# Seven products for eight: Strassen's scheme over pairs of weight blocks in a four-mixer decoder layer

## The chip, the cores and the metric

The kernel runs on one core of one Trainium2 chip. The metric is the device time of one execution in microseconds (us), and lower is better. The work of a core is spread over TensorE (PE: matmuls; PEld is its loading of the stationary operand), VectorE (DVE), ScalarE (ACT) and GpSimd (POOL), with DMA queues that SyncE (SP) and GpSimd fill. Each engine takes its instructions in program order and waits on semaphores for the others.

## The reference

One pre-norm residual layer over 256 tokens of width 2048, in float32. What matters here is the shape of the products: `h @ w_in` is 256 x 2048 by 2048 x 17,492, four branch products are 256 x 512 by 512 x 2048, and the output projection is 256 x 2048 by 2048 x 2048.

```python
h = rms_norm(x, norm_w)
p = h @ w_in
z, gate, dsa_qkv, idx_q, idx_k, idx_w, fox_qkv, fox_f, diff_qkv, dil_qkv = split(p)
branches = (dsa_attention(...), forgetting_attention(...),          # 4 heads of 128
            differential_attention(...), dilated_attention(...))
for b in range(4):
    y = branches[b] * silu(z_parts[b])                              # 256 x 512
    term = sigmoid(g_parts[b]) * (y @ w_branch[b])                  # 256 x 2048
    merged = term if merged is None else merged + term
x = x + merged @ w_out
return rms_norm(x, final_norm_w)
```

The first mixer scores all keys with a 16-head indexer and keeps the best 64. The second adds cumulative log forget gates. The third is the difference of two softmaxes a head. The fourth is a dilated window. Three of them add a position bias.

## The kernel before

Every product has float32 precision made of two parts: an operand is split in a high part (rounded to the format that TensorE multiplies at full rate) and a low part (the rest), and high x high, low x high and high x low are summed in PSUM. The activations are split once (`hT`, 16 chunks of 128 input columns by 256 tokens). The weights pass by in units: a `Unit` is a block of 4 chunks of 128 rows by 512 columns, 1 MB. `load` issues its DMA on the SP queue into one of four buffers `raw`; `split` lets ScalarE copy the high part `whi` (L134) and VectorE subtract it to get the low part `wlo` (L135). High and low parts have three buffers each (`SPLIT + 1`).

There are two forms of products. In token form (`tok_units`, L273 to L275) the activations are stationary and the weights stream by, 512 columns at a time: 4 chunks x 2 token blocks x 3 products are 24 matmuls a unit. The values, the gates, the branch products and the output projection have this form. In transposed form (`T_units`, L278 and L283) the weights are stationary, and the results come out as [column, token]: 16 matmuls of 512 columns and 16 of 256. The index queries, queries, keys and gate path `z` have it; its two halves are added by `add_halves` (L317, L320), with a copy by ScalarE, and GpSimd multiplies by 1/rms.

All units stand in one list `units`, and the last loop of `body` goes through it. At unit i it issues in this order: `split` of unit i+2, `load` of unit i+6, the matmuls of unit i, its evictions (`post`), and one step of every active thread (`run_threads`). Threads hold the attention: `head_thread` and `diff_thread` are started behind the values and take a step after every unit; a step may be logits and softmax, the transposes, or the product with the values. So each engine's queue holds split, eviction and attention work in the order of the units, and nothing is reordered. Per branch there are 16 units of queries, keys, z and values (12 of them in transposed form), 16 of gates and 4 of the branch product. The output projection has 16.

## Time and profile before

| | |
|---|---|
| runs shown | 999.53, 999.70, 1001.15 us; median 999.7 us |
| the profiled execution's span, first to last instruction | 997.9 us |
| busy: TensorE, VectorE, ScalarE, GpSimd | 989.2, 559.9, 467.6, 92.5 us |
| moved by DMA | 187.42 MB, mean 188 GB/s |

The profile lists one span and no separate time of its own execution; the median of the runs is 1.8 us above the span. Busy time counts what an engine executes, not its waits. In the rows below a timeline row gives the start and the duration in us, the engine, the line, the operation and its operands (out<-in, by the program's names); "[3.93 <-ACT whi L134]" is idle time of the engine just before and what ended it.

### The profile page before, as it was taken

The page shows a single profiled execution, that of the slowest core. Times are in us where ns is not written, and L with a number is a line of the kernel's source. Part 1 is how long each engine was busy: PE and PEld are TensorE (multiplying, and loading weights), DVE is VectorE, ACT ScalarE, POOL GpSimd, SP SyncE. Part 2 cuts the span into 40 slices and gives each one's busy share as a digit, 9 for nine tenths or more (in the row PEclk, how much of TensorE's full clock was granted, in tenths as well). Part 3 has the DMA queues.
Part 4 walks back from the last instruction along what each step waited for, and adds up shares of the span by engine and source line. Part 5 has one row for each costly group of instructions (what it writes and reads, how often), then busy time and mean ns, then how long its engine had stood idle before and what let it go on. Part 6 is the DMA issues. An engine that isn't in the chain of part 4 may idle for free.

```text
span 997.9 us, 11965 instructions
## 1 busy us (share of the span) xinstructions
PE 989.2 (99%) x4935; PEld 833.2 (83%) x4935; DVE 559.9 (56%) x642; ACT 467.6 (47%) x502; POOL 92.5 (9%) x87
## 2 busy tenths in 40 slices
PE   9999999999999999999999999999999999999996
PEld 8888888888888888888888877888888888888886
DVE  5767777554556545545555455648454555366443
ACT  5764555543434355534343455643434454444441
POOL 2022010000001100002200000004000000031110
PEclk9999999999999999999999999999999999999999
DMA  9765555565656565556565645565565555855632
GB/s 322 225 212 201 196 173 170 170 207 174 227 175 205 169 199 181 169 170 206 178 204 170 206 133 168 169 193 186 172 202 185 178 173 187 310 196 169 194 102 85
DMA packets 97687, 187.42 MB, mean 188 GB/s; under 512 B 7507, under 2 KB 9717, under 8 KB 97248
## 3 DMA queue, kind: packets, MB, share of 16 engines
q1 hardware_dynamic: 96240, 181.06, 55.0%
q0 software_dynamic: 1360, 5.59, 1.5%
q8 instruction: 39, 0.64, 0.2%
q14 instruction: 16, 0.13, 0.0%
q10 hardware_dynamic: 32, 0.01, 0.0%
HBM read 184.52 MB, written 2.12 MB: 187 GB/s over the span
## 4 chain that ended last, share of the span: by engine, by line
PE 99%; issue 1%; ACT 0%; POOL 0%; DVE 0%; POOLq 0%; ACTq 0%
PE ps_g L273 12%; PE ps_g L275 12%; PE ps_g L274 12%; PE ps_q L278 6%; PE ps_k L278 6%; PE ps_z L278 6%; PE ps_z L283 3%; PE ps_q L283 3%; PE ps_k L283 3%; PE ps_iq L278 3%; PE ps_v L273 3%; PE ps_v L275 3%; PE ps_b L273 3%; PE ps_b L275 3%; PE ps_v L274 3%; PE ps_b L274 3%
## 5 line engine op out<-in xcount | busy, mean ns | idle before, releaser
L135 DVE TENSOR_TENSOR wlo<-raw,whi 128x2048 fp32r<-128x2048 f32 (+3 forms) x175 | 400.5, 2290 | 336.6 <-ACT whi L134 336.6
L134 ACT ACTIVATE whi<-raw 128x2048 fp32r<-128x2048 f32 (+3 forms) x175 | 321.6, 1841 | 273.2 <-issue 48.5
L273 PE MATMUL ps_g<-whi,hT 128*128 128x512 f32 x512 | 204.9, 400 | 0.0
L275 PE MATMUL ps_g<-wlo,hT 128*128 128x512 f32 x512 | 199.7, 390 | 0.0
L274 PE MATMUL ps_g<-whi,hT 128*128 128x512 f32 x512 | 199.7, 390 | 0.0
L273 PEld LDWEIGHTS ps_g<-whi,hT 128*128 128x128 f32 x512 | 96.2, 188 | 21.7 <-issue 2.0
L275 PEld LDWEIGHTS ps_g<-wlo,hT 128*128 128x128 f32 x512 | 96.2, 188 | 20.6
L274 PEld LDWEIGHTS ps_g<-whi,hT 128*128 128x128 f32 x512 | 96.3, 188 | 19.0
L278 PE MATMUL ps_q<-hT,whi 128*128 128x512 f32 x256 | 91.0, 400 | 0.0
L278 PE MATMUL ps_k<-hT,whi 128*128 128x512 f32 x256 | 90.8, 399 | 0.0
L278 PE MATMUL ps_z<-hT,whi 128*128 128x512 f32 x256 | 90.7, 399 | 0.0
L283 PE MATMUL ps_z<-hT,wlo 128*128 128x256 f32 x256 | 71.9, 281 | 0.0
L283 PE MATMUL ps_k<-hT,wlo 128*128 128x256 f32 x256 | 71.9, 281 | 0.0
L283 PE MATMUL ps_q<-hT,wlo 128*128 128x256 f32 x256 | 71.9, 281 | 0.0
L278 PEld LDWEIGHTS ps_q<-hT,whi 128*128 128x128 f32 x256 | 48.1, 188 | 12.5 <-issue 0.6
L278 PEld LDWEIGHTS ps_z<-hT,whi 128*128 128x128 f32 x256 | 48.1, 188 | 11.8
L278 PEld LDWEIGHTS ps_k<-hT,whi 128*128 128x128 f32 x256 | 48.1, 188 | 11.9
L273 PE MATMUL ps_b<-whi,yT 128*128 128x512 f32 x128 | 49.9, 390 | 0.0
L273 PE MATMUL ps_v<-whi,hT 128*128 128x512 f32 x128 | 49.9, 390 | 0.0
L275 PE MATMUL ps_v<-wlo,hT 128*128 128x512 f32 x128 | 49.8, 389 | 0.0
L275 PE MATMUL ps_b<-wlo,yT 128*128 128x512 f32 x128 | 49.8, 389 | 0.0
L274 PE MATMUL ps_v<-whi,hT 128*128 128x512 f32 x128 | 49.8, 389 | 0.0
(208 smaller groups left out, 1269.6 us busy)
## 6 DMA issues: line engine op xcount, KB each, us to landing
raw<-in_w_in_dram SPq DMA_DIRECT2D x132, 1024.0 KB, 4.9
raw<-in_w_branch_dram SPq DMA_DIRECT2D x16, 1024.0 KB, 4.9
raw<-in_w_out_dram SPq DMA_DIRECT2D x16, 1024.0 KB, 5.0
raw<-in_w_in_dram SPq DMA_DIRECT2D x7, 512.0 KB, 10.6
xs<-in_x_dram SPq DMA_DIRECT2D x8, 256.0 KB, 8.1
xf<-in_x_dram POOLq DMA_DIRECT2D x2, 1024.0 KB, 8.7
bt<-vdr POOLq DMA_DIRECT2D x1, 1664.0 KB, 11.3
out_dram<-xf SPq DMA_DIRECT2D x5, 256.0 KB, 2.8
```

The lines of the kernel that those rows point to most:

```text
L134: nc.scalar.activation(u.hi[:, s_], raw[:, s_], AF.Copy)
L135: nc.vector.tensor_tensor(u.lo[:, s_], raw[:, s_], u.hi[:, s_].bitcast(F32), op=ALU.subtract)
L273: nc.tensor.matmul(ps, ahi[:, ts_], u.hi[:, k, cols], start=first, stop=False)
L274: nc.tensor.matmul(ps, alo[:, ts_], u.hi[:, k, cols], start=False, stop=False)
L275: nc.tensor.matmul(ps, ahi[:, ts_], u.lo[:, k, cols], start=False, stop=last)
L278: nc.tensor.matmul(ps[:m], u.hi[:, k, j * P:j * P + m], hT[:, k0 + k].rearrange("p a s -> p (a s)"), start=k0 + k == 0, stop=False)
L283: nc.tensor.matmul(ps[:m, :S], u.lo[:, k, j * P:j * P + m], hT[:, k0 + k, 0], start=False, stop=k0 + k == KC - 1)
```

## The change

Strassen's scheme (in Winograd's form) multiplies two 2 x 2 block matrices with seven block products in place of eight. Here the left matrix is the activations: two blocks of 128 tokens by two blocks of 4 chunks, the first 8 of the 16 chunks. The right one is weights: those 8 chunks by a pair of 512-column blocks, B11, B12 in the first four chunks and B21, B22 in the next four. The other 8 chunks are multiplied as before. 17 pairs are treated so: per branch queries with keys, gate path with values, and two pairs of gates; and the first pair of the output projection.

`seven` gives the 11 units of a pair: seven products of 4 chunks by one token block (12 matmuls each: u1, u5, u3, u6, u7, u2, u4) and four plain units c2a, c2b, c1a, c1b (24 matmuls). Four units have a sum ahead of them (`pre`), which VectorE adds in place in the raw weight buffers; `sums` is issued for unit i+3, behind the split of unit i+2. The sums of the activations are made once for the input (`act_forms` on `hT`) and once for the merged result. The four PSUM banks of a pair keep running sums, which are read in between: `Tok`, `Gate` and `Out` say by which engine. Queries, keys and gate path now come out in token form and are transposed on TensorE by `turn`. The raw buffers become five named slots, and a load is issued when the split that frees its slot has been issued. The bias table is fetched branch by branch and read in reverse order, so that the reversing copies on GpSimd go; the adds into `m` move from GpSimd to VectorE.

The core of the diff:

```diff
+class Raw:
+    def __init__(self, slot, src, k0, nk, c0, n):
+        self.slot, self.src, self.k0, self.nk, self.c0, self.n = slot, src, k0, nk, c0, n
...
 class Unit:
-    """A block of weights (nk chunks of 128 rows by n columns) and the products that use it."""
-    def __init__(self, src, k0, nk, c0, n, mm, post=(), need=(), start=()):
-        self.src, self.k0, self.nk, self.c0, self.n = src, k0, nk, c0, n
+    def __init__(self, raw, mm, post=(), need=(), start=(), pre=(), frees=None, loads=None):
+        self.raw, self.k0, self.nk, self.n = raw, raw.k0, raw.nk, raw.n
         self.mm, self.post = mm, list(post)
-        self.need, self.start = list(need), list(start)
+        self.need, self.start, self.pre = list(need), list(start), list(pre)
+        self.frees = [raw] if frees is None else list(frees)
+        self.loads = [raw] if loads is None else list(loads)
...
+    def free(raws):
+        for r in raws:
+            if waiting[r.slot]:
+                load(waiting[r.slot].popleft())
+    def sums(u):
+        for to, of in u.pre:
+            nc.vector.tensor_tensor(to.tile, to.tile, of.tile, op=ALU.add)
...
     def split(u, hi=None, lo=None, parts=1, part=None):
         if not part:
...
+        raw = u.raw.tile[:, :u.nk * u.n].rearrange("p (k n) -> p k n", k=u.nk)
         for i in range(0, u.nk, step) if part is None else (part * step,):
             s_ = slice(i, i + step)
             nc.scalar.activation(u.hi[:, s_], raw[:, s_], AF.Copy)
             nc.vector.tensor_tensor(u.lo[:, s_], raw[:, s_], u.hi[:, s_].bitcast(F32),
                                     op=ALU.subtract)
+        if part is None or part == parts - 1:
+            free(u.frees)
...
+    def act_forms(T, pool, tag):
+        V["sf"] = big.tile([P, 2, 8, 2, P], F32R, name="sf", tag="sf")
+        a = pool.tile([P, 2, 8, P], F32, name="asum", tag=tag)
+        for t in range(2):
+            c = T[:, 0:8, :, t * P:(t + 1) * P].bitcast(F32)
+            nc.vector.tensor_tensor(a[:, t], c[:, :, 0], c[:, :, 1], op=ALU.add)
+        yield
+        a11, a12, a21, a22 = a[:, 0, 0:4], a[:, 0, 4:8], a[:, 1, 0:4], a[:, 1, 4:8]
+        nc.vector.tensor_tensor(a22, a21, a22, op=ALU.subtract)
+        nc.vector.tensor_tensor(a21, a11, a21, op=ALU.subtract)
+        nc.vector.tensor_tensor(a11, a22, a11, op=ALU.subtract)
+        nc.vector.tensor_tensor(a12, a11, a12, op=ALU.add)
+        for t in range(2):
+            nc.scalar.activation(V["sf"][:, t, :, 0], a[:, t], AF.Copy)
+            nc.vector.tensor_tensor(V["sf"][:, t, :, 1], a[:, t],
+                                    V["sf"][:, t, :, 0].bitcast(F32), op=ALU.subtract)
+    def seven(src, c1, c2, base, ev, name, need=(), start=()):
+        st = {}
+        B11, B12 = Raw(0, src, 0, 4, c1, 512), Raw(1, src, 0, 4, c2, 512)
+        B21, B22 = Raw(3, src, 4, 4, c1, 512), Raw(2, src, 4, 4, c2, 512)
+        def whole(half, k0):
+            t = slice(half * P, (half + 1) * P)
+            return lambda k: (base()[:, k0 + k, 0, t], base()[:, k0 + k, 1, t])
+        def form(half, k0):
+            return lambda k: (V["sf"][:, half, k0 + k, 0], V["sf"][:, half, k0 + k, 1])
+        def product(bank, act, first=False):
+            def mm(u):
+                if first:
+                    st[bank] = main_ps(name)
+                for k in range(4):
+                    three(st[bank], act(k), u, k, first and k == 0, k == 3, on=True)
+            return mm
+        def plain(k0, two):
+            def mm(u):
+                for t, bank in enumerate(two):
+                    new = bank not in st
+                    if new:
+                        st[bank] = main_ps(name)
+                    act = whole(t, k0)
+                    for k in range(4):
+                        three(st[bank], act(k), u, k, new and k == 0, k == 3, on=True)
+            return mm
+        def c(k0, c0, two):
+            return Unit(Raw(4, src, k0, 4, c0, 512), plain(k0, two))
+        def read(f, bank, last=False):
+            def g():
+                f(st[bank])
+                if last:
+                    done(st[bank])
+            return g
+        u1 = Unit(B11, product("Y", whole(0, 0), True), loads=[B11, B12, B22, B21], frees=[],
+                  post=[read(ev.p1, "Y")], need=need)
+        u5 = Unit(B11, product("W", form(1, 4), True), loads=[], frees=[], pre=[(B11, B12)],
+                  post=[read(ev.p5, "W")])
+        c2a = c(8, c2, "ZW")
+        u3 = Unit(B22, product("Z", form(0, 4)), loads=[], frees=[], pre=[(B12, B22)])
+        u6 = Unit(B22, product("Y", form(0, 0)), loads=[], frees=[B11], pre=[(B22, B11)],
+                  post=[read(ev.u2, "Y")])
+        c2b = c(12, c2, "ZW")
+        c2b.post += [read(ev.c12, "Z", True)]
+        u7 = Unit(B12, product("Y", form(1, 0)), loads=[], post=[read(ev.u3, "Y")])
+        u2 = Unit(B21, product("X", whole(0, 4), True), loads=[], frees=[],
+                  post=[read(ev.c22, "W", True)])
+        c1a = c(8, c1, "XY")
+        u4 = Unit(B21, product("Y", whole(1, 4)), loads=[], frees=[B22, B21], pre=[(B21, B22)])
+        c1b = c(12, c1, "XY")
+        c1b.post += [read(ev.c11, "X", True), read(ev.c21, "Y", True), ev.end]
+        c1b.start += start
+        return [u1, u5, c2a, u3, u6, c2b, u7, u2, c1a, u4, c1b]
...
+    class Tok:
+        def __init__(self, dst, s1, s2, end):
+            self.dst, self.s1, self.s2, self.end = dst, s1, s2, end
+        def p1(self, ps):
+            self.d1, self.d2 = self.dst()
+            nc.scalar.activation(self.d1[:, 0], ps, AF.Copy, scale=self.s1[:, 0:1])
+        def p5(self, ps):
+            nc.scalar.activation(self.d2[:, 0], ps, AF.Copy, scale=self.s2[:, 0:1])
+        def u2(self, ps):
+            d = self.d2[:, 0]
+            nc.vector.scalar_tensor_tensor(d, ps, self.s2[:, 0:1], d, op0=ALU.mult,
+                                           op1=ALU.subtract)
+        def u3(self, ps):
+            nc.scalar.activation(self.d2[:, 1], ps, AF.Copy, scale=self.s2[:, 1:2])
+        def c12(self, ps):
+            d = self.d2[:, 0]
+            nc.vector.scalar_tensor_tensor(d, ps, self.s2[:, 0:1], d, op0=ALU.mult,
+                                           op1=ALU.subtract)
+        def c22(self, ps):
+            d = self.d2[:, 1]
+            nc.vector.scalar_tensor_tensor(d, ps, self.s2[:, 1:2], d, op0=ALU.mult,
+                                           op1=ALU.subtract)
+        def c11(self, ps):
+            d = self.d1[:, 0]
+            nc.vector.scalar_tensor_tensor(d, ps, self.s1[:, 0:1], d, op0=ALU.mult, op1=ALU.add)
+        def c21(self, ps):
+            nc.scalar.activation(self.d1[:, 1], ps, AF.Copy, scale=self.s1[:, 1:2])
+    class Gate(Tok):
+        def c12(self, ps):
+            super().c12(ps)
+            nc.scalar.activation(self.d2[:, 0], self.d2[:, 0], AF.Sigmoid)
+        def c22(self, ps):
+            super().c22(ps)
+            nc.scalar.activation(self.d2[:, 1], self.d2[:, 1], AF.Sigmoid)
+        def c11(self, ps):
+            super().c11(ps)
+            nc.scalar.activation(self.d1[:, 0], self.d1[:, 0], AF.Sigmoid)
+        def c21(self, ps):
+            nc.scalar.activation(self.d1[:, 1], ps, AF.Sigmoid, scale=self.s1[:, 1:2])
...
     def qkvz_units(b, off, scale, start):
-        def ev_q(ps):
+            if b == 0:
+                if "tok" not in V:
+                    V["tok"] = big.tile([P, 4, 2, 512], F32, name="tok", tag="m")
+                return V["tok"][:, names == "zv"], V["tok"][:, 2 + (names == "zv")]
+            return [big.tile([P, 2, 512], F32, name="tok", tag="g", bufs=4) for _ in range(2)]
+        def dst_qk():
+            V["q_"], V["k_"] = d = two("qk")
+            return d
+        def dst_zv():
+            V["z_"] = two("zv")[0] if b == 0 else big.tile([P, 2, 512], F32, name="tok", tag="g",
+                                                           bufs=4)
+            V["v"] = at.tile([P, 2, 512], F32, name="v", tag="v")
+            return V["z_"], V["v"]
+        def turn(src, dst, j0):
+            for j in range(0, 4, 2):
+                tp = att_ps("turn")
+                for i in range(2):
+                    for t in range(2):
+                        nc.tensor.transpose(tp[:, i * S + t * P:i * S + (t + 1) * P],
+                                            src[:, t, (j + i) * P:(j + i + 1) * P], ident)
+                nc.scalar.activation(dst[:, j0 + j:j0 + j + 2],
+                                     tp.rearrange("p (i s) -> p i s", i=2), AF.Copy)
+                yield
+        def qk_thread():
             V["qk"] = at.tile([P, 8, S], F32, name="qk", tag="qk")
-            ev_half(ps, 0, scale)
-        def ev_half(ps, i, sc):
-            for j in range(4):
-                add_halves(V["qk"][:, 4 * i + j], ps[j], sc)
-            part = V["qk"][:, 4 * i:4 * i + 4]
-            nc.gpsimd.tensor_tensor(part, part, rows4(), op=ALU.mult)
-        def ev_v(ps):
-            V["v"] = at.tile([P, 2, 512], F32, name="v", tag="v")
-            for t in range(2):
-                nc.scalar.activation(V["v"][:, t], ps[t], AF.Copy, scale=rst[:, t:t + 1])
-        def ev_z(ps):
+            q_, k_ = V["q_"], V["k_"]
+            yield from turn(q_, V["qk"], 0)
+            yield from turn(k_, V["qk"], 4)
+        def z_thread():
+            z_ = V["z_"]
+            sg = big.tile([P, 2, 512], F32, name="sg", tag="g", bufs=4)
+            nc.scalar.activation(sg, z_, AF.Sigmoid)
+            nc.vector.tensor_tensor(z_, z_, sg, op=ALU.mult)
+            yield
             V["sz"] = at.tile([P, 4, S], F32, name="sz", tag="sz")
-            for j in range(4):
-                add_halves(V["sz"][:, j], ps[j])
-            nc.gpsimd.tensor_tensor(V["sz"], V["sz"], rows4(), op=ALU.mult)
-        def silu_thread():
-            sg = big.tile([P, 4, S], F32, name="sg", tag="g", bufs=4)
-            yield
-            nc.scalar.activation(sg, V["sz"], AF.Sigmoid)
-            yield
-            nc.vector.tensor_tensor(V["sz"], V["sz"], sg, op=ALU.mult)
-        return (T_units(off, ev_q, "ps_q") + T_units(off + 512, lambda ps: ev_half(ps, 1, None), "ps_k")
-                + T_units(O_Z + b * 512, ev_z, "ps_z", start=[silu_thread])
+        return (seven(w_in, off, off + 512, lambda: hT, Tok(dst_qk, sc, rst, end), "ps_qk",
+                      start=[("qk", qk_thread)])
+                + seven(w_in, O_Z + b * 512, off + 1024, lambda: hT, Tok(dst_zv, rst, rst, end),
+                        "ps_zv", start=[z_thread] + start))
     ki_hi = at.tile([P, S], F32R, name="ki_hi")
     ki_lo = at.tile([P, S], F32R, name="ki_lo")
-    kiT = at.tile([64, S], F32, name="kiT", tag="t256", bufs=5)
+    kiT = at.tile([64, S], F32, name="kiT", tag="t256", bufs=4)
...
-    def gate_units(b, n):
-        def ev(ps):
-            g = big.tile([P, 2, 512], F32, name="g", tag="g", bufs=4)
-            V["g"][n] = g
-            for t in range(2):
-                nc.scalar.activation(g[:, t], ps[t], AF.Sigmoid, scale=rst[:, t:t + 1])
-        return tok_units(w_in, O_G + b * D + n * 512, h_act, KC, ev, "ps_g")
+    def gate_units(b, i):
+        def dst():
+            for n in (2 * i, 2 * i + 1):
+                V["g"][n] = big.tile([P, 2, 512], F32, name="g", tag="g", bufs=4)
+            return V["g"][2 * i], V["g"][2 * i + 1]
+        c = O_G + b * D + 2 * i * 512
+        return seven(w_in, c, c + 512, lambda: hT, Gate(dst, rst, rst, lambda: None), "ps_g")
...
             nc.vector.tensor_tensor(mT[:, c:c + 2, 1], src, mT[:, c:c + 2, 0].bitcast(F32),
                                     op=ALU.subtract)
+        if n == 1:
...
-                    nc.gpsimd.tensor_tensor(m[:, n, t], m[:, n, t], g[:, t], op=ALU.add)
-        return tok_units(w_branch[b], n * 512, lambda k: (V["yT"][:, k, 0], V["yT"][:, k, 1]), 4, ev,
+                    nc.vector.tensor_tensor(m[:, n, t], m[:, n, t], g[:, t], op=ALU.add)
+        return tok_units(w_branch[b], n * 512, lambda k: (V["yT"][:, k, 0], V["yT"][:, k, 1]),
+                         (0, 1, 4, 2)[n:n + 1], ev,
                          "ps_b", need=[f"att{b}"] if n == 0 else [],
                          start=[lambda: merge_thread(n)] if b == 3 else [])
...
+    class Out:
+        def add(self, ps, t, c, op=ALU.add):
+            d = V["xf"][:, t, c * 512:(c + 1) * 512]
+            if op is ALU.add:
+                nc.vector.tensor_tensor(d, d, ps, op=op)
+            else:
+                nc.vector.tensor_tensor(d, d, ps, op=ALU.subtract)
...
+        def c12(self, ps):
+            out_col(ps, 0, 512, 512, 1)
...
     for b, off, scale, fn in ((0, O_DSA, HSCALE, head_thread), (1, O_FOX, HSCALE, head_thread),
                               (2, O_DIFF, 0.125, diff_thread), (3, O_DIL, HSCALE, head_thread)):
         units += qkvz_units(b, off, scale, att_threads(b, fn))
-        for n in range(4):
-            units += gate_units(b, n)
+        for i in range(2):
+            units += gate_units(b, i)
         for n in range(4):
             units += branch_units(b, n)
         if b == 0:
             units[-1].start.append(fox_thread)
+        elif b < 3:
+            units[-1].post.append(lambda b=b: new_bias(4 * b))
     last_gate = len(units) - 5
     units[last_gate + 1].post.insert(0, open_final)
-    for n in range(4):
-        units += out_units(n)
-    # startup: x and the first weights by pairs of chunks, the tensor engine kept awake
+    units += seven(w_out, 0, 512, lambda: V["mT"], Out(), "ps_o")
+    units += out_units(2, (0, 1, 4, 2))
+    units += out_units(3, (3, 0, 1, 4))
...
         split(units[i])
-        load(units[i + RAW_BUFS])
     for i in range(RAMP, len(units)):
         u = units[i]
         if i + SPLIT < len(units):
             v_ = units[i + SPLIT]
             if getattr(v_, "keep", False):
-                split(v_, V["mg"].tile([P, 2048], F32R, name="hi4"),
-                      V["mg"].tile([P, 2048], F32R, name="lo4"))
+                kept = big.tile([P, 2, 2048], F32R, name="kept", tag="m")
+                split(v_, kept[:, 0], kept[:, 1])
             else:
                 split(v_)
-        if i + SPLIT + RAW_BUFS < len(units):
-            load(units[i + SPLIT + RAW_BUFS])
+        if i + SPLIT + 1 < len(units):
+            sums(units[i + SPLIT + 1])
         while any(a[0] in u.need for a in active):
```

## Rows read from the trace of the kernel before

**Rows 1.** The page, parts 1 and 2: TensorE's busy row and its clock.
```profile
PE 989.2 (99%) x4935; PEld 833.2 (83%) x4935; DVE 559.9 (56%) x642; ACT 467.6 (47%) x502; POOL 92.5 (9%) x87
...
PEclk9999999999999999999999999999999999999999
```
**Rows 2.** The page, part 4: the chain that ended last, by engine.
```profile
PE 99%; issue 1%; ACT 0%; POOL 0%; DVE 0%; POOLq 0%; ACTq 0%
```
**Rows 3.** Windows, one for each branch: window, length, busy us, clock, DMA.
```profile
60.40:276.00 215.60, 215.60 (x1086) 181.91 (x1085) 141.56 (x208) 109.05 (x116) 14.43 (x13) 1.00 0.56 186
276.00:481.40 205.40, 205.40 (x1006) 172.96 (x1005) 110.41 (x105) 91.75 (x88) 14.84 (x9) 1.00 0.56 184
481.40:693.50 212.10, 212.10 (x1038) 175.60 (x1037) 116.10 (x141) 100.14 (x122) 21.96 (x19) 1.00 0.55 179
693.50:899.70 206.20, 206.20 (x1013) 173.71 (x1012) 108.23 (x100) 92.63 (x89) 19.09 (x14) 1.00 0.59 199
```
**Rows 4.** Timeline of PE, ACT and DVE in one attention step, 370 to 378 us.
```profile
371.06 0.82 PE L496 MATMUL lps<-qk 128*128 128x128 f32 x4
...
372.79 0.40 ACT L515 ACTIVATE lg<-lg,mx 128x128 f32<-128x128 f32 x1 [3.18 <-DVE mx L513]
...
373.69 1.90 ACT L134 ACTIVATE whi<-raw 128x2048 fp32r<-128x2048 f32 x1
...
375.62 2.29 DVE L135 TENSOR_TENSOR wlo<-raw,whi 128x2048 fp32r<-128x2048 f32 x1 [2.86 <-ACT whi L134]
```
**Rows 5.** Timeline of PE: one token-form stretch, one transposed-form stretch.
```profile
225.93 0.39 PE L274 MATMUL ps_g<-whi,hT 128*128 128x512 f32 x1
...
226.61 0.39 PE L274 MATMUL ps_g<-whi,hT 128*128 128x512 f32 x1
...
299.68 0.40 PE L278 MATMUL ps_k<-hT,whi 128*128 128x512 f32 x1
...
301.09 0.40 PE L278 MATMUL ps_k<-hT,whi 128*128 128x512 f32 x1
```
**Rows 6.** Timeline of PE at a merge's eight transposes.
```profile
893.40 1.03 PE L640 MATMUL mtp<-ident,m 128*128 128x128 f32 x8
894.19 0.48 PE L273 MATMUL ps_b<-whi,yT 128*128 128x512 f32 x1
```
**Rows 7.** Groups by line and shape: count, busy us, mean ns, idle before.
```profile
L135 DVE TENSOR_TENSOR wlo<-raw,whi 128x2048 fp32r<-128x2048 f32 x161 | 384.4, 2388 | 332.2 <-ACT whi L134 332.2
L134 ACT ACTIVATE whi<-raw 128x2048 fp32r<-128x2048 f32 x161 | 307.9, 1913 | 273.2 <-issue 48.5 <-PE ps_b L274 43.3 <-PE ps_z L278 35.4
...
L627 ACT ACTIVATE g<-ps_g,rst 128x512 f32<-128x512 f32 x32 | 21.2, 687 | 22.7 <-PE ps_g L275 22.6
...
L657 DVE TENSOR_TENSOR g<-ps_b,g 128x512 f32<-128x512 f32 x24 | 16.1, 683 | 0.8 <-PE ps_b L275 0.4
L135 DVE TENSOR_TENSOR wlo<-raw,whi 128x1024 fp32r<-128x1024 f32 x11 | 13.3, 1225 | 4.4 <-ACT whi L134 4.4
...
L317 DVE TENSOR_TENSOR qk<-ps_k,halves 128x256 f32<-128x256 f32 x16 | 6.0, 417 | 3.0 <-ACT halves L316 3.0
...
L681 ACT ACTIVATE sq<-xf 128x512 f32<-128x512 f32 x7 | 4.4, 632 | 18.0 <-DVE xf L679 18.0
...
L134 ACT ACTIVATE whi<-raw 128x512 fp32r<-128x512 f32 x2 | 1.1, 620 | 0.0
```
**Rows 8.** Timeline, GpSimd adding beside a low part on DVE.
```profile
888.15 2.55 POOL L658 TENSOR_TENSOR m<-m,g 128x512 f32<-128x512 f32 x2 [2.83 <-DVE g L657]
...
889.88 2.96 DVE L135 TENSOR_TENSOR wlo<-raw,whi 128x2048 fp32r<-128x2048 f32 x1 [1.04 <-ACT whi L134]
```
**Rows 9.** Waits: who waited for whom, us in total, times, longest.
```profile
DVE wlo L135 <- ACT whi L134: 336.6, 157, 4.2
```
**Rows 10.** The page, part 6: the weight loads, us from issue to landing.
```profile
raw<-in_w_in_dram SPq DMA_DIRECT2D x132, 1024.0 KB, 4.9
```

177 lines of the change are left out of this document (110 added, 67 removed).

## The prediction, made before the change was run

> **What bounds the kernel now.** I read the page first: the TensorE row and the clock row [rows 1]. The reader is to see an engine that is busy for 99% of the span at full granted clock, and a VectorE at 56%. The chain of work that ended last says the same [rows 2]: every step leads back to a matmul. The windows by branch [rows 3] show that this holds everywhere: in each of the four branches TensorE's busy time equals the length of the window, while VectorE is busy for 52 to 66% of it. So two things have to be costed: TensorE's time, which the change cuts, and VectorE's and ScalarE's time, which it raises and which costs nothing today.
>
> How much room do the other two have? They work in a fixed order, written out by the program: at unit i, ScalarE makes the high part of unit i+2, VectorE its low part, and then both read unit i's results and serve the attention threads. A high part can't start before TensorE has finished unit i-1, since there are three buffers. An attention step shows the whole path [rows 4]: TensorE leaves a unit at 371.06 and starts the logits, the exponentials begin at 372.79, the next high part at 373.69, and its low part ends at 375.62 + 2.29 = 377.91. That is 6.85 us after the unit's end, and it is hidden, because two units of 24 matmuls follow. Three matmuls start 0.68 us apart in token form (225.93 to 226.61 [rows 5]), 0.2267 us each, so two units last 2 x 5.44 = 10.9 us.
>
> **What TensorE gains.** A pair took 8 units of 24 matmuls, 192; it will take 7 x 12 + 4 x 24 = 180. Per branch there are four pairs: 48 matmuls fewer, 48 x 0.2267 = 10.9 us. The 12 units of queries, keys and gate path change form: in the old form a 512- and a 256-column matmul take (301.09 - 299.68) / 4 = 0.3525 us [rows 5], 16 of them 5.64 us, against 5.44 us in token form: 12 x 0.20 = 2.4 us less. For it 24 transposes of 128x128 come back. Eight transposes kept TensorE for 894.19 - 893.40 = 0.79 us [rows 6], so 24 cost 2.4 us. Net 10.9 us a branch, 43.6 us for four, and 12 x 0.2267 = 2.7 us in the output projection. If TensorE stayed the bound, the kernel would take 46 us less.
>
> **What VectorE gets, per branch.** Durations are those of [rows 7]. Removed: 12 additions of halves at 0.42, 5.0 us. Added: each pair is split in 11 units and not in 8, so 12 more low parts, and it has four sums of weight blocks, 16 per branch. A sum isn't in this trace; the nearest row is the low part, with the same shape, both operands in SBUF. I take its undisturbed 2.29 [rows 4] for the 28 of them, 64.1 us. From below, ScalarE's 1.91 for the same block would make it 53.5; from above, the mean of 2.388 makes it 66.9. Four evictions a pair go to VectorE (the differences of products), nearest row 0.683, 16 of them 10.9 us; these carry a scalar operand too, and a tenth more for it would be 1 us. The adds into m move from GpSimd to VectorE in three branches, 8 x 0.683 = 5.5 us. Together 64.1 + 10.9 + 5.5 - 5.0 = 75.5 us (70.0 in the first branch). GpSimd's removed work gives a little back: a low part beside it took 2.96 us [rows 8]; the mean of 2.388 falls to 2.29, over 144 old low parts 14.1 us in all. The reversed reading of the bias I take at no cost: the same elements are read once, and if it halved VectorE's rate it would add some 0.7 us a head, 3 us a branch.
>
> **What VectorE waits for, per branch.** Today it idles 336.6 us before low parts, waiting for ScalarE [rows 9], at no cost, as TensorE is slower. After the change it isn't slower, and these waits stand in VectorE's own queue. Three sums of a pair (for u5, u6 and u4) write the block that is split next: VectorE sums, ScalarE must make the high part, 1.91 us [rows 7], VectorE waits, with nothing else to do, then subtracts. With two hand-overs of 0.03 us (373.69 + 1.90 to 375.62 [rows 4]) that is 2.0 us each, 12 per branch, 24 us. In the two gate pairs the sigmoid no longer reads PSUM: VectorE combines first, ScalarE takes the sigmoid of the result, and the next high part is queued behind it on ScalarE, and behind that the next low part. At c12 and c22 that is 0.62 to 0.69 + 1.91 = 2.6 us, at the pair's end two sigmoids, 3.2 us: 8.4 us a pair, 16.8 us a branch. Together 40.8 us. The differential branch also runs eight softmaxes instead of four; each puts exponentials of 0.9 us (372.79 to 373.69 [rows 4]) ahead of a high part, 7.2 us. In the other branches these lie beside low parts that VectorE still owes, and I take nothing.
>
> **The sum.** VectorE's busy time of before [rows 3] plus these: first branch 141.6 + 70.0 + 40.8 = 252.4; second 110.4 + 75.5 + 40.8 = 226.7; third 116.1 + 75.5 + 40.8 + 7.2 = 239.6; fourth 108.2 + 75.5 + 40.8 = 224.5. That is 943.2, less 14.1, 929.1 us, against TensorE's windows of 215.6 + 205.4 + 212.1 + 206.2 = 839.3 us. VectorE's path is the longer in each branch: 89.8 us are lost. TensorE has less to hide it with: two short units last 5.44 us, a short and a long one 8.16, and must cover the 6.85 us of [rows 4] plus a sum of 2.29.
>
> The output projection's pair has 15 x 2.29 + 8 x 0.683 + 3 x 2.0 on VectorE, and squares of 0.63 us on ScalarE ahead of high parts [rows 7], 2 x (0.63 + 1.91) + 2 x 0.63 + 1.91 = 8.3: 54.2 us against 8 x 5.44 = 43.5 before, 10.7 us lost. The activation sums of the merged result are 4 x 1.225 + 4 x 0.683 = 7.6 us on VectorE [rows 7] just ahead of it; half of it I take as exposed, 4 us (bounds 0 and 7.6). The same sums for the input lie under the index queries, where TensorE has 5.6 us units and VectorE room: nothing.
>
> Transfers: 8 blocks a pair, as before, each 4.9 us to landing [rows 10]. Slot 4 serves c1a and c1b in turn: the load goes out behind c1a's low part, and a sum, a wait and a low part (2.29 + 2.0 + 2.29 = 6.6 us) lie before the block is needed. Hidden; without that cover 4.9 us a pair. The bias rows come by GpSimd's queue a whole projection ahead: hidden.
>
> The profiled execution has a span of 997.9 us; the median of the runs shown is 999.7, 1.8 more. 997.9 + 89.8 + 10.7 + 4 = 1102.4, and with the 1.8 us around it **1104 us**.
>
> **The rivals.** *TensorE stays the bound.* ScalarE might run far enough ahead that VectorE never waits. VectorE's work alone is then 252.4 - 40.8 - 3.5 = 208 us in the first branch, and the others follow TensorE's 194.5, 201.2 and 195.3: 799 us, and with 2.7 us from the output, 957 us. For it: VectorE's pure work fits in three branches. Against it: in a sum followed by the split of its own result, and in a combine followed by a sigmoid, nothing is there to run ahead with. It decides at the waits: in the second branch 226.7 - 3.5 - 40.8 = 182.4 us are work, so the change loses as long as more than 23 of the 40.8 us of waits are exposed.
>
> *Half the waits are filled* by attention steps and evictions that happen to fall there: 4 x 20.4 us less, some 1,025 us. For it: a branch has 108.2 - 36 x 2.388 - 5.0 - 5.5 = 11.7 us of attention and silu work on VectorE, some of which will fall into waits. Against: it is concentrated in one pair of four.
>
> *The clock falls.* The granted clock was 1.00, that is 2.4 GHz, in each window [rows 3], and TensorE had no gap to speak of. After the change the first gate pair of a branch holds 40.8 us of matmuls in some 63 us (34.4 + 2.7 + 6.0 = 43.1 of a plain pair, 8.4 of sigmoids, some 11 of attention and silu), in gaps of 2 to 5 us. With its matmuls at 1.2 GHz it would take 82. Three of these by 19 us and the third branch's, longer by its 7.2 us, by 12 are 69 us; three quarters of it gives 1,156 us. The Trainium skill ("TensorE: Matmul & The Clock Gate", on HAM oscillation) says that gaps in the work throttle the clock again, which is this rival; by it the sum would be up to 1,173 us. No gap of before lets the trace agree or differ.
>
> **How the numbers follow.** 0.62 for the forecast, by its bounds 1,065 to 1,140; 0.13 for half the waits, around 1,025; 0.11 for TensorE staying the bound; 0.14 for the clock. The range is 1,015 to 1,165: it leaves out the faster case and the upper end of the clock's. Faster by over 0.2%, which is about what a measurement of this kernel can tell from no change, 0.11; within 0.2%, 0.03; slower, 0.86.
>
> **What would show it.** TensorE's share falls to some 86% and VectorE's rises to near 80%; the chain that ended last goes through VectorE's sums and low parts and ScalarE's high parts. VectorE's waits for high parts come right after sums, near 2 us each; ScalarE waits for sums and for combined gates. A gate pair without attention takes some 51 us, one with it over 60, a pair of queries and keys 43. Wrong would be: TensorE at 95% or more, gate pairs of 41 us, or a granted clock under 0.95.

## The result and the profile after

The changed kernel takes 1127.6 us (median of 1126.6 to 1130.4) against 999.8 us: a ratio of 1.128, with a 95% interval of 1.127 to 1.130. It is slower by 128 us, where the forecast was 1104.

The page of the changed kernel: the busy rows, TensorE's clock in 40 slices, the chain that ended last.

```profile
PE 1000.9 (89%) x4443; PEld 806.5 (72%) x4443; DVE 852.0 (76%) x821; ACT 584.9 (52%) x581; POOL 32.4 (3%) x51
...
PEclk9989999989999999899999897899999999996999
...
DVE 37%; PE 34%; ACT 16%; issue 10%; DMA 2%; ACTq 0%; POOL 0%; POOLq 0%; DVEq 0%
DVE wlo L171 19%; ACT whi L170 13%; DVE raw L156 10%; PE ps_zv L321 3%; PE ps_zv L322 3%; PE ps_zv L323 3%; PE ps_g L323 2%; PE ps_o L323 2%; PE ps_o L321 2%; PE ps_o L322 2%; PE ps_g L322 2%; PE ps_g L321 2%; PE ps_b L322 2%; PE ps_b L321 2%; DMA raw<-in_w_in_dram 2%
```

TensorE has gone from 99% to 89% of a longer span [rows 1], and the chain that was all matmuls [rows 2] now goes back mostly through low parts, high parts and sums (L171, L170, L156). No engine is busy all the time. That is the picture of a bound made of work and waits in one queue.

Windows of the changed kernel: one for each branch, then the output stage (window, length, busy us of PE, PEld, DVE, ACT, POOL, granted clock, DMA share, GB/s).

```profile
62.10:315.10 253.00, 222.03 (x966) 177.54 (x965) 203.89 (x242) 138.13 (x136) 3.81 (x7) 0.95 0.47 155
315.10:538.40 223.30, 203.93 (x887) 164.38 (x886) 175.01 (x144) 118.76 (x105) 0.78 (x1) 0.97 0.51 172
538.40:780.00 241.60, 216.54 (x917) 170.90 (x916) 182.61 (x182) 127.18 (x139) 7.14 (x9) 0.94 0.48 159
780.00:1007.60 227.60, 204.15 (x901) 164.33 (x900) 175.49 (x142) 120.72 (x109) 1.63 (x3) 0.99 0.53 180
1007.60:1117.00 109.40, 95.60 (x437) 78.24 (x435) 69.03 (x58) 41.92 (x40) 9.07 (x8) 0.91 0.34 116
```

The same window of the output stage in the kernel before:

```profile
899.70:990.40 90.70, 90.58 (x457) 76.91 (x455) 44.07 (x39) 35.63 (x37) 11.64 (x10) 1.00 0.43 140
```

The branches add up to 945.5 us against 839.3 [rows 3]: 106.2 us lost. The output stage takes 109.4 us against 90.7, 18.7 lost, and the first branch starts 1.7 us later. That is the whole difference of the spans, 126.6 us.

VectorE's waits in the second branch, then in the whole run (engine, line, waited for: us in total, times, longest).

```profile
DVE wlo L171 <- ACT whi L170: 46.6, 23, 3.1
DVE yT L757 <- ACT yT L756: 1.6, 1, 1.6
```

```profile
DVE wlo L171 <- ACT whi L170: 227.3, 116, 4.6
...
ACT whi L170 <- DVE raw L156: 195.7, 44, 7.5
```

In the second branch 175.0 us of work and 48.2 us of waits make 223.2 of the 223.3 us. VectorE's waits there are all for ScalarE, nearly all for its high parts, and ScalarE's in turn, in the whole run, are mostly for VectorE's sums. In all VectorE waits less for high parts than before (227.3 us against 336.6 [rows 9]); the same kind of wait that cost nothing then is on the path now.

Inside that branch: queries, keys, z and values, then the gates, first of the changed kernel, then of the kernel before.

```profile
315.20:402.60 87.40, 84.65 (x378) 68.67 (x377) 73.64 (x47) 46.66 (x33) 0.00 (x0) 1.00 0.57 193
402.60:516.60 114.00, 97.38 (x413) 77.63 (x412) 82.80 (x80) 63.36 (x68) 0.78 (x1) 0.94 0.46 155
```

```profile
276.00:365.60 89.60, 89.60 (x481) 76.82 (x480) 49.39 (x38) 36.22 (x30) 7.20 (x3) 1.00 0.58 188
365.60:459.60 94.00, 94.00 (x429) 78.07 (x428) 45.36 (x56) 47.21 (x52) 0.00 (x0) 1.00 0.55 179
```

So Strassen's scheme even gains 2.2 us over the first two pairs, and loses 20 over the two gate pairs. The timeline of VectorE in the second of these, without attention (start, duration, line, operation; in brackets the idle time before it and what ended it):

```profile
480.13 2.29 DVE L156 TENSOR_TENSOR raw<-raw 128x2048 f32<-128x2048 f32 x1
484.46 6.69 DVE L171 TENSOR_TENSOR wlo<-raw,whi 128x2048 fp32r<-128x2048 f32 x3 [2.04 <-ACT whi L170]
...
493.93 0.74 DVE L482 SCALAR_TENSOR_TENSOR g<-ps_g,rst,g 128x512 f32<-128x512 f32 x1
497.18 2.29 DVE L171 TENSOR_TENSOR wlo<-raw,whi 128x2048 fp32r<-128x2048 f32 x1 [2.50 <-ACT whi L170]
499.39 2.28 DVE L156 TENSOR_TENSOR raw<-raw 128x2048 f32<-128x2048 f32 x1
503.71 2.29 DVE L171 TENSOR_TENSOR wlo<-raw,whi 128x2048 fp32r<-128x2048 f32 x1 [2.04 <-ACT whi L170]
505.92 0.74 DVE L487 SCALAR_TENSOR_TENSOR g<-ps_g,rst,g 128x512 f32<-128x512 f32 x1
509.17 6.70 DVE L171 TENSOR_TENSOR wlo<-raw,whi 128x2048 fp32r<-128x2048 f32 x3 [2.50 <-ACT whi L170]
515.78 0.74 DVE L492 SCALAR_TENSOR_TENSOR g<-ps_g,rst,g 128x512 f32<-128x512 f32 x1
519.60 2.29 DVE L171 TENSOR_TENSOR wlo<-raw,whi 128x2048 fp32r<-128x2048 f32 x1 [3.08 <-ACT whi L170]
```

VectorE in the first gate pair, where attention runs and ScalarE also makes the exponentials of each head's softmax:

```profile
422.47 2.29 DVE L171 TENSOR_TENSOR wlo<-raw,whi 128x2048 fp32r<-128x2048 f32 x1 [1.32 <-ACT whi L170]
...
428.38 2.29 DVE L171 TENSOR_TENSOR wlo<-raw,whi 128x2048 fp32r<-128x2048 f32 x1 [2.86 <-ACT whi L170]
...
443.94 2.29 DVE L171 TENSOR_TENSOR wlo<-raw,whi 128x2048 fp32r<-128x2048 f32 x1 [1.52 <-ACT whi L170]
```

The first of these follows a sum and the third a combine; their waits are shorter, because small attention operations stand in them. The second follows neither: its high part is queued behind a head's exponentials.

And ScalarE in the second pair, behind the combine at 493.93:

```profile
494.71 0.63 ACT L502 ACTIVATE g<-g 128x512 f32<-128x512 f32 x1 [3.61 <-DVE g L482]
495.24 1.90 ACT L170 ACTIVATE whi<-raw 128x2048 fp32r<-128x2048 f32 x1
```

Both hand-overs of the prediction stand here: a sum (L156), then 2.04 us until its high part is there; a combine (L482), its sigmoid (L502), the high part behind it, and 2.50 us until VectorE may go on. What stays open is whether these waits are what the kernel loses, and which of them.

### The profile page after: what moved, and what is told of

Its sections match the earlier page's. It is cut to its first block, busy times and chain, and to the rows that moved or that the text cites. A ratio compares the mean times of both kernels' runs of the same rounds, so it can differ in the third digit from the quotient of the medians.

```text
span 1124.5 us, 11339 instructions
## 1 busy us (share of the span) xinstructions
PE 1000.9 (89%) x4443; PEld 806.5 (72%) x4443; DVE 852.0 (76%) x821; ACT 584.9 (52%) x581; POOL 32.4 (3%) x51
## 4 chain that ended last, share of the span: by engine, by line
DVE 37%; PE 34%; ACT 16%; issue 10%; DMA 2%; ACTq 0%; POOL 0%; POOLq 0%; DVEq 0%
DVE wlo L171 19%; ACT whi L170 13%; DVE raw L156 10%; PE ps_zv L321 3%; PE ps_zv L322 3%; PE ps_zv L323 3%; PE ps_g L323 2%; PE ps_o L323 2%; PE ps_o L321 2%; PE ps_o L322 2%; PE ps_g L322 2%; PE ps_g L321 2%; PE ps_b L322 2%; PE ps_b L321 2%; DMA raw<-in_w_in_dram 2%
## 5 line engine op out<-in xcount | busy, mean ns | idle before, releaser
L171 DVE TENSOR_TENSOR wlo<-raw,whi 128x2048 fp32r<-128x2048 f32 (+2 forms) x226 | 499.0, 2219 | 227.8 <-ACT whi L170 227.3
L170 ACT ACTIVATE whi<-raw 128x2048 fp32r<-128x2048 f32 (+2 forms) x226 | 415.2, 1853 | 283.9 <-DVE raw L156 195.7
L323 PE MATMUL ps_g<-wlo,hT 128*128 128x512 f32 x352 | 144.8, 411 | 17.0 <-DVE wlo L171 16.9
L156 DVE TENSOR_TENSOR raw<-raw 128x2048 f32<-128x2048 f32 x68 | 155.6, 2288 | 1.2
L321 PE MATMUL ps_g<-whi,hT 128*128 128x512 f32 x352 | 149.2, 424 | 3.7 <-ACT whi L170 3.7
L322 PE MATMUL ps_g<-whi,hT 128*128 128x512 f32 x352 | 143.9, 409 | 0.0
L321 PE MATMUL ps_qk<-whi,hT 128*128 128x512 f32 x176 | 70.4, 400 | 4.4 <-ACT tok L470 4.4
L323 PE MATMUL ps_qk<-wlo,hT 128*128 128x512 f32 x176 | 69.8, 397 | 0.0
L323 PE MATMUL ps_zv<-wlo,hT 128*128 128x512 f32 x176 | 68.9, 392 | 1.0 <-DVE wlo L171 1.0
L322 PE MATMUL ps_qk<-whi,hT 128*128 128x512 f32 x176 | 69.8, 396 | 0.0
L321 PE MATMUL ps_zv<-whi,hT 128*128 128x512 f32 x176 | 68.9, 392 | 0.0
L322 PE MATMUL ps_zv<-whi,hT 128*128 128x512 f32 x176 | 68.5, 389 | 0.0
L321 PE MATMUL ps_g<-whi,sf 128*128 128x512 f32 x128 | 54.1, 423 | 2.2 <-ACT whi L170 2.2
L322 PE MATMUL ps_g<-whi,sf 128*128 128x512 f32 x128 | 51.1, 400 | 0.0
```

The source lines that it names most:

```text
L156: nc.vector.tensor_tensor(to.tile, to.tile, of.tile, op=ALU.add)
L170: nc.scalar.activation(u.hi[:, s_], raw[:, s_], AF.Copy)
L171: nc.vector.tensor_tensor(u.lo[:, s_], raw[:, s_], u.hi[:, s_].bitcast(F32), op=ALU.subtract)
L321: nc.tensor.matmul(ps, ahi, u.hi[:, k, cols], start=first, stop=False, skip_group_check=on)
L322: nc.tensor.matmul(ps, alo, u.hi[:, k, cols], start=False, stop=False, skip_group_check=on)
L323: nc.tensor.matmul(ps, ahi, u.lo[:, k, cols], start=False, stop=last, skip_group_check=on)
```

## The experiments

The medians of before beside these runs were 999.5 to 1000.6 us. Cuts in the code are marked by "..." or by a comment.

**Without the seven products.** The token form alone: two calls of plain units for a pair, in the output projection too, and no sums of activations.

```diff
+        pair = plain_pair                 # 2 x tok_units, ScalarE evicts
...
-        return (seven(w_in, off, off + 512, ...
+        return (pair(w_in, off, off + 512, ...
...
-        return seven(w_in, c, c + 512, lambda: hT, Gate(...
+        return plain_pair(w_in, c, c + 512, lambda: hT, Gate(...
...
-    units[4].start += [lambda: act_forms(hT, at, "qk")]
```

> Every pair of blocks is computed as eight plain units in token form; the seven products, the weight sums and the sums of activations are gone, the token form of queries, keys and gate path, their 24 transposes a branch and the reversed reading of the bias stay. If Strassen's extra work on VectorE and its waits are what costs, TensorE is the bound again and the time is that of before, 995 to 1,012 us, with TensorE near 99% and a clock of 1.00. Rival, the token form and its transposes cost a good part of the 128 us: the time stays above 1,040.

Measured: 1001.0 us, ratio 1.0012 [1.0002, 1.0021]. Its page:

```profile
PE 989.5 (99%) x4647; PEld 822.7 (82%) x4647; DVE 535.5 (54%) x618; ACT 478.9 (48%) x502; POOL 31.3 (3%) x51
```

The change of form, the transposes, the reversed bias and the moved adds together cost 1 us; the rest of the loss belongs to the seven products and what they bring with them.

**Only the gates plain.** `gate_units` returns `plain_pair`, whose sigmoid reads PSUM again; all else as changed.

> The eight gate pairs are computed plainly in token form, the sigmoid reading PSUM; the seven products stay for queries and keys, z and values, and the output. If the loss is per pair of VectorE's queue, with a gate pair's own sigmoid waits on top, the eight gate pairs carry most of it: 1,025 to 1,040. Rival, the loss is spread evenly over the 17 pairs: half of it, 128 x 8/17 = 60 us, comes back, 1,067.

Measured: 1034.9 us, ratio 1.034 [1.033, 1.036]. Eight of 17 pairs carry 93 of the 128 us. Of what is left, the first branch's first two pairs lose 14.3 us (114.2 us from their first matmul to the first of the gates, against 99.9 before), though the same two pairs gain in the second branch; the first branch's indexer runs beside them. Most of the rest lies in the output stage. The second branch, in the same two windows as above:

```profile
293.30:380.50 87.20, 84.48 (x378) 68.65 (x377) 74.03 (x47) 47.82 (x33) 0.00 (x0) 1.00 0.56 199
380.50:475.20 94.70, 94.70 (x437) 78.83 (x436) 46.50 (x57) 49.13 (x55) 0.78 (x1) 1.00 0.55 189
```

**Only the output plain.** `out_units` for all four column blocks, no `act_forms` of the merged result.

> Only the output projection goes back to plain units; the sums of the merged result go with it. The output stage took 109.4 us in the changed kernel against 90.7 before, so the theory that the losses of the stages add up expects 1,127.6 - 18.7 = 1,109, and from the prediction's own terms (10.7 + 4) 1,113. Rival, the stage's loss was carried into it from the last branch: above 1,120.

Measured: 1111.6 us, ratio 1.112 [1.110, 1.114], 16.0 us less, where the windows gave 18.7 for the stage. The losses of the stages add up to within some 3 us, and the executions of either kernel spread over 4 to 5.

**No weight sums.** The body of `sums` becomes `pass`, so the products take blocks that were not summed.

> The 68 sums of weight blocks are left out (the products then use the wrong blocks), all else stays: seven products, 11 splits a pair, evictions on VectorE, sigmoids after the combines. If the sums and the waits behind them are the main cost, VectorE loses 16 x 2.21 = 35 us of work and up to 12 x 2.04 = 24 us of waits a branch. Counted in full that puts VectorE below TensorE's 799 us for the four branches, and the kernel near 975; with the sigmoids' waits still in the queue, which the order of the units doesn't let it make up, near 1,020. Rival, short units of 2.7 us or the lower clock hold TensorE back by themselves: above 1,090.

Measured: 1018.9 us, ratio 1.019 [1.017, 1.020]. 109 us go, with short units still in place, and the kernel stays 19 us above before. Sums and what hangs on them are most of the loss. This run takes VectorE's work (702.0 us busy against 852.0) and its waits away at once; the next ones part them.

**Halved sums and splits.** The same elements, in two instructions each, for the three blocks of a pair that are summed and then split.

```diff
         for to, of in u.pre:
-            nc.vector.tensor_tensor(to.tile, to.tile, of.tile, op=ALU.add)
+            n = 1024 if to is u.raw else 2048
+            for c in range(0, 2048, n):
+                nc.vector.tensor_tensor(to.tile[:, c:c + n], ..., op=ALU.add)
...
+            if v_.pre and v_.pre[0][0] is v_.raw:
+                split(v_, parts=2)
```

> The three sums of a pair whose result is split next, and the splits of those blocks, are made in two halves each. VectorE's elements and their order stay; only ScalarE can make the first half's high part while VectorE sums the second, and the second half's while VectorE subtracts the first. If the wait of 2.04 us behind each such sum is the cost, most of 4 x 12 x 2.04 = 98 us of waits goes, though part of it turns up ahead of other low parts: 1,085 to 1,095 by the queues followed step by step. Rival, the elements that VectorE handles set the time: 1,127 or, with 102 more operations, a little over.

Measured: 1082.2 us, ratio 1.083 [1.081, 1.084]: 45.4 us less with VectorE's elements unchanged (it is busy for 859.7 us against 852.0). VectorE at a sum that is split next, and then its window of queries and keys in the second branch:

```profile
461.19 2.36 DVE L159 TENSOR_TENSOR raw<-raw 128x1024 f32<-128x1024 f32 x2
463.60 2.36 DVE L175 TENSOR_TENSOR wlo<-raw,whi 128x1024 fp32r<-128x1024 f32 x2
466.48 4.49 DVE L175 TENSOR_TENSOR wlo<-raw,whi 128x2048 fp32r<-128x2048 f32 x2 [0.52 <-ACT whi L174]
```

```profile
305.00:345.80 40.80, 40.80 (x181) 33.72 (x181) 37.45 (x32) 22.74 (x17) 0.00 (x0) 1.00 0.61 206
```

The low part follows the sum without the 2.04 us of [2.04 <-ACT whi L170] above. And a pair that VectorE no longer holds up takes 40.8 us, which is 180 x 0.2267: Strassen's gain, in full, in one place. Only half of the 98 us comes back. VectorE's waits for high parts in the whole run:

```profile
DVE wlo L175 <- ACT whi L174: 171.6, 99, 4.6
```

They fell by 55.7 us from 227.3 and not by 98, and the 102 more operations add 7.7 us of work; that comes near the 45.4. Part of the removed waits turned up ahead of other low parts, like the 0.52 us above. Another part may stand where VectorE gets ahead of TensorE, as in this pair, and a shorter wait is worth nothing; the runs don't part the two.

**Late sigmoids.** The sigmoid of a combined gate is issued one unit later.

```diff
+        def late(self, d):
+            def g():
+                yield
+                nc.scalar.activation(d, d, AF.Sigmoid)
+            active.append(("", g()))
-            nc.scalar.activation(self.d2[:, 0], self.d2[:, 0], AF.Sigmoid)   # and two more
+            self.late(self.d2[:, 0])
```

> The three sigmoids of a gate pair that follow a combine on VectorE are issued one unit later, behind the next high part instead of ahead of it. The prediction priced their place in the queue at 8.4 us a pair, 67 us in all: 1,060 us by that. Following the queues step by step with the durations of the trace, part of it comes back as other waits, and some 28 us are gained: 1,100 us. Rival, the waits at the combines come from elsewhere (TensorE's late products): within 5 us of 1,128.

Measured: 1107.1 us, ratio 1.107 [1.106, 1.109], 20.5 us less: neither 67 nor nothing. VectorE and ScalarE at the same combines (L482, L487) show why:

```profile
487.93 0.74 DVE L482 SCALAR_TENSOR_TENSOR g<-ps_g,rst,g 128x512 f32<-128x512 f32 x1
491.18 2.29 DVE L171 TENSOR_TENSOR wlo<-raw,whi 128x2048 fp32r<-128x2048 f32 x1 [2.51 <-ACT whi L170]
...
499.93 0.74 DVE L487 SCALAR_TENSOR_TENSOR g<-ps_g,rst,g 128x512 f32<-128x512 f32 x1
500.61 2.29 DVE L171 TENSOR_TENSOR wlo<-raw,whi 128x2048 fp32r<-128x2048 f32 x1
```

```profile
489.24 1.92 ACT L170 ACTIVATE whi<-raw 128x2048 fp32r<-128x2048 f32 x1 [3.54 <-PE ps_g L322]
```

Behind L487 the wait is gone. Behind L482 it is as long as before, with another end: the high part now waits for TensorE to leave its buffer. The sigmoid stood in the shadow of that. Whether a fourth buffer for high and low parts would shorten this wait wasn't tried.

**Work in the gap, work beside it.** 48 spare reductions, 1.478 us each, in two places.

```diff
             sums(units[i + SPLIT + 1])
+            if units[i + SPLIT + 1].fill == "in":    # u5, u6, u4; in the other run "out": c2a, u2, c1b
+                filler()    # nc.vector.reduce_sum of `ones`, 128x1280 elements
```

> 48 more VectorE operations (a reduction of 128x1280 elements, about 1.4 us each, some 67 us in all) stand right behind the sums, three a pair, in the gap in which VectorE waits for the high part of the block just summed. If that gap of 2.0 us is a wait of VectorE in its own queue, most of it is swallowed: 1,140 to 1,150. Rival, VectorE's work as such sets the time and the waits are only slack: 1,127 plus 67, 1,195.

> The same 48 operations, three a pair, but ahead of low parts that follow no sum. If VectorE's work and waits add up in one queue, work put where it doesn't wait is added nearly in full: 1,175 to 1,195. Rival, VectorE has slack or TensorE sets the time: below 1,150 and the same as with the operations in the gap.

Measured: 1142.4 us in the gap (14.8 more), 1193.2 us beside it (65.6 more); ratios 1.141 [1.139, 1.144] and 1.193 [1.191, 1.195]. The groups of low parts and fillers, first in the gap, then beside it (count, busy us, mean ns, idle before):

```profile
L172 DVE TENSOR_TENSOR wlo<-raw,whi 128x2048 fp32r<-128x2048 f32 x212 | 482.8, 2287 | 172.7 <-ACT whi L171 172.5 <-PE ps_ix L688 0.2
...
L186 DVE TENSOR_REDUCE fill<-ones 128x10 f32<-128x1280 f32 x48 | 70.9, 1478 | 0.0
```

```profile
L172 DVE TENSOR_TENSOR wlo<-raw,whi 128x2048 fp32r<-128x2048 f32 x212 | 482.8, 2288 | 226.0 <-ACT whi L171 225.6 <-PE ps_zv L330 0.4
```

The changed kernel has 223.1 us of idle time ahead of the same 212 low parts. In the gap the 70.9 us of fillers take 50.4 us of it; beside it they take none, and nearly all of them is added. The same work has two prices, by its place in the queue.

**Sums on GpSimd.** `nc.vector` becomes `nc.gpsimd` in `sums`.

> The weight sums go to GpSimd: VectorE loses 68 x 2.21 = 150 us of work. If VectorE's share of busy time were what counts, the kernel would come down toward 1,020. If the serial chain sum, high part, low part counts, a sum of some 4.8 us (twice the 2.40 us that GpSimd took for half such a block) in place of 2.29 makes each of 12 chains a branch longer, and low parts beside it slow from 2.29 to 2.96: 1,140 to 1,200, slower although VectorE does less.

Measured: 1236.2 us, ratio 1.236 [1.234, 1.238]: slower though VectorE has less to do, as the chain says, and above the range. The sum was sized about right, at 4.8 us for 4.593; VectorE beside it was not:

```profile
L156 POOL TENSOR_TENSOR raw<-raw 128x2048 f32<-128x2048 f32 x68 | 312.3, 4593 | 719.3 <-DVE wlo L171 429.2 <-issue 240.0 <-DVE sm L773 37.7
```

```profile
L171 DVE TENSOR_TENSOR wlo<-raw,whi 128x2048 fp32r<-128x2048 f32 x212 | 544.1, 2583 | 356.9 <-ACT whi L170 356.3
L875 DVE TENSOR_TENSOR m<-m,g 128x512 f32<-128x512 f32 x24 | 40.1, 1672 | 0.8
```

VectorE is busy for 828.0 us, against 702.0 in the run without sums: what the sums gave up came back as longer operations. It idles 356.9 us ahead of these low parts, against 223.1.

**The clock.** First TensorE with a third less to do, then with spare products in its gaps.

```diff
-        nc.tensor.matmul(ps, alo, u.hi[:, k, cols], start=False, stop=False, ...)
+        if not on:      # on: the units of `seven`
+            nc.tensor.matmul(ps, alo, u.hi[:, k, cols], start=False, stop=False)
```

```diff
+        if u.fill:      # u5, u6, u4
+            wake = att_ps("wake")
+            for _ in range(8):
+                nc.tensor.matmul(wake[:, :P], ones, ones, start=True, stop=True)
         u.mm(u)
```

> The product of the activations' low part with the weights' high part is left out in all seven-product pairs, so TensorE does a third less there: 60 matmuls a pair, 17 x 60 x 0.2267 = 231 us less at full clock. If VectorE's queue sets the time, it stays near 1,120 to 1,135, and TensorE's share falls to some 70%. Rival, TensorE at a falling clock carries a good part of the loss: below 1,090.

> Eight spare 128x128 products, some 1.7 us, go to TensorE ahead of each product that follows a weight sum (48 places), where it stands idle anyway. If VectorE's queue sets the time, the granted clock rises from 0.956 toward 0.99 and the time moves by less than 12 us either way. Rival, the clock is a good part of the loss: with it restored 20 to 40 us are gained, 1,088 to 1,108.

Measured: 1122.1 us with two products, ratio 1.123 [1.121, 1.125]; 1144.3 us with spare ones, 1.144 [1.142, 1.146]. The page with two products:

```profile
PE 859.1 (77%) x3423; PEld 664.6 (59%) x3423; DVE 852.3 (76%) x821; ACT 583.1 (52%) x581; POOL 32.3 (3%) x51
...
DVE 44%; PE 21%; ACT 19%; issue 13%; DMA 1%; ACTq 0%; POOL 0%; POOLq 0%; DVEq 0%
```

TensorE loses 142 us of busy time, its mean granted clock falls further, from 0.956 to 0.872, and the kernel takes 5.5 us less. With levels of 1.2 and 2.4 GHz these means are some 99 and 287 us of the span at the lower one. A third of the products less in the 17 pairs and three times as long at the lower clock change the time by half a percent: neither TensorE's work nor its clock sets it. The spare products were a miss: the clock came up only to 0.968 and the time rose by 17 us, with TensorE now 64% of the chain. My reading is that they were too much for the gaps; this run alone decides nothing about the clock.

**A mixed version.** Seven products only for queries, keys, z and values of the last three branches and the second gate pair of all but the third branch, with halved sums and late sigmoids; plain pairs elsewhere.

> A candidate: seven products only where VectorE has nothing else to serve (queries and keys, z and values of the last three branches, the second gate pair of all but the third branch), with halved sums and late sigmoids; plain units in token form in the first branch's projections, wherever attention runs, and in the output. If theory holds that VectorE's serial waits and its attention work are what Strassen's gain is lost to, these nine pairs follow TensorE and each saves up to 12 x 0.2267 = 2.7 us: 25 us less than token form alone, 972 to 985. Rival, each Strassen pair still costs more than it saves: above 1,000.

Measured: 989.0 us, ratio 0.989 [0.988, 0.991]: 1.1% under before and faster than both kernels, but 4 us above the range. Its second and fourth branch:

```profile
273.80:472.70 198.90, 197.66 (x897) 163.71 (x896) 157.83 (x149) 113.87 (x108) 0.78 (x1) 1.00 0.57 193
...
681.10:890.60 209.50, 203.17 (x917) 167.21 (x916) 159.41 (x148) 115.53 (x111) 1.63 (x3) 0.98 0.58 201
```

```profile
ACT whi L174 <- DMA raw<-in_w_in_dram: 17.2, 4, 10.2
```

The second branch gains 6.5 us on before [rows 3], the first and third 2.0 and 3.7; the fourth loses 3.3, with 17.2 us of high parts waiting for weight loads, the longest 10.2. That plain and Strassen pairs take up the five slots in another order is my reading of it; a better order wasn't tried.

## Why the prediction was right, and where it was off

The mechanism held: VectorE's queue, its work and its waits together, became the bound. The second branch came out at 223.3 us for 223.2 (226.7 less a quarter of 14.1), but that is luck: two errors cancel, the work was 175.0 us and not 182.4, the waits 48.2 and not 40.8. The 2.29 us of an operation was right, its cost in a row too high: three low parts stand in 6.69 us, so each starts 2.20 after the last. Over the four branches the same holds: work of 737.0 us for 758.7, idle time of 208.5 for 170.4. The forecast was nearer than its terms.

The 23.6 us that were missing lie in the waits above all. The branches came to 945.5 us against 929.1. Waits for high parts measured 43.3, 46.6, 58.0 and 49.7 us a branch where the terms were 40.8, 40.8, 48.0 and 40.8. Away from attention the priced waits were right: 2.04 us behind a sum, and a gate pair's three (2.50, 2.50, 3.08, together 8.1 for 8.4). What was mis-sized is a head's exponentials, which were priced in the third branch alone and taken at nothing in the others, to lie beside low parts that VectorE still owes. In the second branch's first gate pair VectorE owes none: each of the four heads puts a wait of 2.85 or 2.86 us into its queue, the exponentials and the high part behind them; one of the four stands where 2.04 had been priced. The output stage lost 18.7 us for 14.7, and 1.7 us came at the head, which had been taken at nothing. The last 1.5 us are rounding and the median, which lies 3.1 us above the profiled span and not 1.8.

As prices of single edits the wait terms don't hold. The sigmoids were put at 67 us and gave back 20.5; the waits behind the sums at 96 and gave back 45.4. A wait that is removed uncovers the next one (TensorE's release of a high part's buffer), or TensorE itself at 40.8 us a pair. The sum came out near because it priced all of them together, and because its errors cancel.

TensorE's gain was right where it could be seen: 2.7 us a pair, in the one pair that takes 40.8 us; the 10.9 us of a whole branch no run shows. Of the signs by stage, 43 us for a pair of queries and keys is near half of 87.4. The two gate pairs had been put at 63 and 51 us and took 65.3 and 48.7 by their matmuls: the 114.0 is right, each part is off by 2.3, the one with attention upward.

*TensorE stays the bound* fell: its share is 89%. *Half the waits are filled* fell, though some were: in the second branch's first gate pair attention filled 0.7 us behind a sum (1.32 for 2.04) and 1.0 behind a combine (1.52 for 2.50), but its exponentials added more than it filled. *The clock falls* happened in part: 0.956 over the span, but 0.94 in the second branch's gates and 0.91 in the output stage, under the 0.95 that was to speak against the forecast. With the clock at 0.872 and a third less to multiply the kernel took 5.5 us less, so the low clock is not what costs the time. The 69 us of that rival didn't come. The Trainium skill ("TensorE: Matmul & The Clock Gate", on HAM oscillation) says that gaps in the work throttle the clock; the 0.956 and 0.872 of these runs agree.

The transfers were hidden nearly as predicted. High parts waited for weight loads in ten places, 14.5 us in all, and in the branches only one such wait reached VectorE, in the fourth branch's gates, with 2.13 us; the 2% of DMA in the chain are mostly loads that ran beside sums and their waits.

## What to carry to other kernels

Saving matmuls is worth what the next engine leaves over: add up that engine's work and its waits in program order before you trade adds for products, and put the trade only into stages where both stay below TensorE. A step that goes from one engine to another and back (sum, high part, low part) is a wait in the first one's queue as long as its own step; cutting it in halves hid much of it here without less work. Price waits as a whole: a single one, taken out, may uncover another. And ask of every other step in the same queue, here a head's exponentials, what it does to them.

## What the runs showed of the hardware

A GpSimd add holds VectorE up until it is done. With the sums on GpSimd an add of m that takes 692 ns by itself averaged 1,672, from 691 to 4,791 ns. One low part beside two sums (the second ends at 332.70 + 9.32 = 342.02), GpSimd first:

```profile
332.70 9.32 POOL L156 TENSOR_TENSOR raw<-raw 128x2048 f32<-128x2048 f32 x2 [31.93 <-DVE wlo L171]
```

```profile
339.30 4.87 DVE L171 TENSOR_TENSOR wlo<-raw,whi 128x2048 fp32r<-128x2048 f32 x1 [4.61 <-ACT whi L170]
```

It starts at 339.30 and ends at 344.17, 2.15 us after the sum's end: it did next to nothing until then. All 26 low parts that started during a sum ended 2.15 us after it, however long they had stood; five operations that read one operand from PSUM (L364, L872, L874) and started during a sum took their usual time. The Trainium skill ("SBUF — State Buffer", who interferes with whom) calls the port that the two share an exclusive lock, held for a whole instruction; this trace agrees for VectorE. That GpSimd is held up in turn no run here shows. The 2.96 us of [rows 8] was a mild case: that low part ended 2.14 us after GpSimd's adds did. The expectation for GpSimd's sums took it for the price, where a low part took up to 6.28 us; that this alone makes the 36 us above its range isn't shown.

A mean granted clock of 0.872 went with a shorter time than one of 0.956. In these runs it went with TensorE's busy share: 0.994 at 98% (the mixed version), 0.956 at 89%, 0.872 at 77%. Read it with the chain before it is called a cost.
